# Where the loads of the value weights stand among the attention's transpositions

## The chip, the cores and the metric

The kernel runs on one core of a Trainium2 chip. The metric is the device time of one execution in microseconds (us), taken as the median of several runs. TensorE (PE in the profile), VectorE (DVE), ScalarE (ACT), GpSimd (POOL) and SyncE (SP) each run their own instructions in order; SP does nothing but issue DMAs.

## The reference

Two pre-norm residual layers over 1024 positions of width 1024, then an RMS norm. The first layer is a gated linear recurrence. The second is attention with a forget gate, and the change lies in it:

```python
u = h @ w_in
q, k, v, gate = ...                        # 16 heads of 64
cum = cumsum(log_sigmoid(f_logit + b_f))   # per head, over positions
logits = q @ k.T / 8 + (cum[q] - cum[k])   # causal
p = softmax(logits)
y = (p @ v) * silu(gate)
x = x + y @ w_out
```

## The kernel before

The attention layer works through the 16 heads one by one, each in two halves of 512 query positions. For a head and a half, `maxima` (L941) makes the scores `S` of four blocks of 128 queries on TensorE, adds the mask and takes the maximum on VectorE (L965), takes the exponential `p` on ScalarE (L970), scales it into two fp16 parts `pp` (ScalarE L978, VectorE L979) and has SP issue a DMA that transposes `pp` into `pT` (L982). So a run of `maxima` has four transpositions. `weigh` (L988) multiplies `pT` with the values into `O`; its first product needs all four transpositions of its half.

`run` (L1034) interleaves such generators by a string of digits and dots: a digit advances a generator (0 is `weigh`, 1 is `maxima`), a dot advances `fill`, the projections that make queries, keys and gates of later heads (`gps`), and `side`, which moves keys and queries into the operands `T` and `U` by DMA (`pieces`, L823, four DMAs for a batch). For each head there are two runs. The second (L1289) weighs the second half of this head and makes the scores of the first half of the next head; its order is

```python
ORDER = "1.1..1.1..00", "1.1.1.1...0000"
```

The values of four heads at a time are made by `values` (L695), for three groups behind the first: after the heads 3, 7 and 11 it is passed to the second run as `vals`, and what is left of it runs when that run is over (`drain(vals)`, L1299). These are the places 1, 2 and 3. The weights of a group come in four tiles of 256 KB from `in_wv`, for k = 0, 2, 4 and 6: `load_v` fetches one into a buffer `wf` (three of them, shared with all weights of the layer, L118), and `cast_v` makes two fp16 parts `w16` of it, the high one on ScalarE and the low one on VectorE (`cast16`, L641). The products go to `vps`: 192 of 128x256, for eight tiles of 128 tokens; the first four token tiles stand in an order that lets work begin with the first weight tiles (L731). A finished token tile is evicted in two halves, each by ScalarE and VectorE (`v`, L761 and L762). Token tiles 0, 2, 4 and 6 use the two banks "g" of PSUM in turn, tiles 1, 3, 5 and 7 the two banks "S", which the scores use too.

Before the change, `run` advances `vals` at three steps: at step 1 (three loads), at step 5 (two casts and the fourth load) and at the last digit 1 (two casts).

The order of instructions on each engine is made by a scheduler when the kernel is built, from the order of the code and its own estimates. `tc.issue_after(i)` keeps what is issued inside behind the instruction `i`. `turns` holds all transpositions so far, so at step 0 of the second run `turns[-1]` and `turns[-2]` are the last two transpositions of the run that has just ended, and at step 1 `turns[-1]` is the first of the new run. `behind` (L1042) keeps the later transpositions behind the fourth load, and the first part of `O`'s eviction (L1010) behind the last cast.

Of the kernel before, what the change touches and what calls it, by code (L numbers as in the profile page):

```python
# [40 lines left out]
def trunk(ctx: ExitStack, tc: tile.TileContext, xt, w0, wg, wo0, pc, gn, gf, w1, wv, wf, bf, wo1, out):  # L41
# [26 lines left out]
    def matmul(*args, **kw):  # L68
        pe[0] = nc.tensor.matmul(*args, **kw)  # L69
        return pe[0]  # L70
# [25 lines left out]
    def to_hi(hi, src, eng, scale=None):  # L96
        if eng is nc.scalar:
            if scale is None:
                cast_last[0] = nc.scalar.copy(hi, src)
            else:  # L100
                nc.scalar.activation(hi, src, AF.Copy, scale=scale)
        elif eng is nc.gpsimd:
            nc.gpsimd.tensor_scalar(hi, src, 1.0 if scale is None else scale, 0.0, ALU.mult, ALU.add)
        elif scale is None:
            eng.tensor_copy(hi, src)
        else:
            eng.tensor_scalar(hi, src, scale, None, ALU.mult)
# [41 lines left out]
    def drain(gen):  # L149
        for _ in gen:  # L150
            pass

    def take(gen, n):
        for _ in range(n):
            next(gen, None)
# [43 lines left out]
    with nullcontext(ExitStack()) as l0:  # L199
# [45 lines left out]
        k = 0  # L245
# [374 lines left out]
    with ExitStack() as l1:  # L620
# [13 lines left out]
        def load16(src, shape, b):  # L634

            wt = loaded(shape)
            for part, sl in src:
                fetch(wt[:, :, sl], part)
            return wt, b

        def cast16(wt, b):  # L641

            n = wt.shape[1]
            both = wpool.tile([P, 2, *wt.shape[1:]], FP16, tag=next(slots), name="w16")
            hi, lo = both[:, 0], both[:, 1]
            cast_last[0] = nc.scalar.activation(hi, wt, AF.Copy, scale=scales[:, b : b + 1])
            nc.vector.scalar_tensor_tensor(lo, wt, scales[:, b : b + 1], hi, ALU.mult, ALU.subtract)
            return [(hi[:, k], lo[:, k]) for k in range(n)]
# [46 lines left out]
        def values(g):  # L695

            ex = HEADS if g == 0 else 0
            parts, raw = [], []

            def load_v(k):  # L700
                src = [(wv[g, :, k : k + 2], slice(0, 256))]
                if ex:
                    src.append((wf[:, k : k + 2], slice(256, 256 + ex)))
                raw.append(load16(src, (2, 256 + ex), g))

            def cast_v(n=1):
                for _ in range(n):
                    parts.extend(cast16(*raw.pop(0)))

            if ex:  # L710
                for k in range(0, KT, 2):
                    load_v(k)
                    if k % 4:
                        cast_v(2)
                    if k == 2:
                        yield
            else:
                for k in range(0, 6, 2):
                    load_v(k)
                yield  # L720
                with tc.issue_after(seen[0].ins):
                    cast_v(2)
                load_v(6)
                yield
                cast_v(2)
                yield
            Vs[2 * g], Vs[2 * g + 1] = [], []
            todo = [(st, k) for st in range(8) for k in range(KT)]
            if not ex:

                todo[: 2 * KT] = [(st, k) for h in range(2) for st in range(2) for k in range(h * 4, h * 4 + 4)]  # L731
            pts = {}
            for st, k in todo:
                if k == 0:
                    if st % 2:
                        pt = ps.tile([P, SEQ], F32, tag="S", name="vps")[:, : 256 + ex]
                    else:
                        pt = ps.tile([P, 256 + ex], F32, tag="g", name="vps")
                    pts[st] = pt
                pt = pts[st]  # L740
                c = (st % 4) * P
                xh, xl = hT[st // 4][k]
                wh, wl = parts[k]
                xh, xl = xh[:, c : c + P], xl[:, c : c + P]
                matmul(pt, xh, wh, start=k == 0, stop=False)
                matmul(pt, xl, wh, start=False, stop=False)
                matmul(pt, xh, wl, start=False, stop=k == KT - 1)
                if k % 4 == 1:
                    yield
                if k < KT - 1:  # L750
                    continue
                if ex and st < 4:
                    take(splitting, 2)
                if True:
                    if ex:
                        nc.vector.tensor_scalar(fz[:, st], pt[:, 256:], rf[:, st : st + 1], None, ALU.mult)
                    for a in range(2):
                        v = vpool.tile([P, 4, HD], FP16, tag=f"v{st}", name=f"v{st}", bufs=2)
                        src = pt[:, a * P : (a + 1) * P].rearrange("p (b d) -> p b d", b=2)
                        rv_ = rv[:, g, st : st + 1]  # L760
                        to_hi(v[:, 0::3], src, nc.scalar, scale=rv_)  # L761
                        nc.vector.scalar_tensor_tensor(v[:, 1:3], src, rv_, v[:, 0::3], ALU.mult, ALU.subtract)  # L762
                        Vs[2 * g + a].append(v)
# [53 lines left out]
        turns = []  # L817
# [41 lines left out]
        def forget(half):  # L859
# [24 lines left out]
            for hd in range(2):  # L884
                if half == 0:
                    load(hd, cs, (0,) if hd == 0 else ())

        first = values(0)
        next(first)
        next(first)  # L890
# [143 lines left out]
        def run(order, *gens, fill=iter(()), side=iter(()), vals=None):  # L1034

            for n, i in enumerate(order):
                if vals and n in (1, 5):
                    with tc.issue_after(turns[-1].ins):
                        next(vals)
                if vals and n == order.rfind("1"):  # L1040
                    next(vals)
                    behind[:] = loaded_last[0], cast_last[0]  # L1042
                with tc.issue_after(pe[0].ins):
                    next(fill if i == "." else gens[int(i)], None)
                if i == ".":
                    next(side, None)
            for g in gens:
                drain(g)
# [196 lines left out]
        load(0, halves[1], (1,))  # L1245
        load(1, halves[1], (1,))
        run("00.0.0", maxima(0, 0), fill=fill)
        load_q(1, 0)
        drain(fill)
        for hd in range(HEADS):  # L1250
# [23 lines left out]
            if hd == HEADS - 1:  # L1274
                first = "1..1.0.1.0.1..."
            side = chain(pieces(hd + 1, 0, 0), pieces(hd + 1, 0, 1)) if hd else iter(())
            run(first, weigh(hd, 0), maxima(hd, 1), fill=fill, side=side)
            drain(side)
            if hd == HEADS - 1:
# [6 lines left out]
            if hd == 14:  # L1286
                side = chain(side, late())
            vals = values(hd // 4 + 1) if hd % 4 == 3 and hd < 12 else None
            run(second, weigh(hd, 1), maxima(hd + 1, 0), fill=fill, side=side, vals=vals)  # L1289
            behind.clear()  # L1290
            drain(side)
# [88 lines left out]
```

## Time and profile before

| | |
|---|---|
| three runs | 1066.57, 1062.53 and 1066.17 us, median 1066.17 |
| the profiled execution | 1067.16 us, span of its instructions 1065.4 us |
| busy in the span | PE 1028.7 us (97%), DVE 784.2 (74%), ACT 659.9 (62%), POOL 92.2 (9%) |
| granted TensorE clock, mean | 0.993 |
| DMA | 148.92 MB in 219805 packets, 161936 of them under 512 bytes |
| value products `vps` | 768, of which 192 in each of the places 1 to 3 |

Times in the profile count from the span's start. A line of the timeline gives start, duration, engine, source line, operation, what is written and read, shape, count, and in brackets how long the engine was idle before and what ended that. SPq is SP's queue of DMA issues; the duration there is that of the issuing, not of the transfer. L57, L66 and L69 are helper lines through which all of ScalarE's activations, the loads and all matmuls go, so groups are told apart by their tiles.

### The profile page before, as it was taken

The numbers are of one execution on the slowest core, as the hardware profiler recorded it, in microseconds if no ns is written. First come the engines' busy times: TensorE is split into PE (matmuls) and PEld (weight loads), VectorE is DVE, ScalarE is ACT, GpSimd is POOL, SyncE is SP. The second block draws the span as 40 slices with busy tenths as digits, with TensorE's granted clock in tenths as the row PEclk, the third lists the DMA queues.
The fourth block names the chain that finished last, engine by engine and source line by source line (L and its number), as shares of the span: only waits on it lengthen the run. The fifth ranks groups of instructions, "written<-read, shape, count | busy, mean of one in ns | idle before, by whom it ended". The sixth has DMA issues, their size and how long they took to land. (4 is left out here: it accounts for less than half of the span.)

```text
span 1065.4 us, 15063 instructions
## 1 busy us (share of the span) xinstructions
PE 1028.7 (97%) x5094; PEld 721.8 (68%) x5094; DVE 784.2 (74%) x1456; ACT 659.9 (62%) x1211; POOL 92.2 (9%) x87
## 2 busy tenths in 40 slices
PE   9999999999999999998999989999999989999997
PEld 6787878888888888765445556554755448577776
DVE  7789667667856868885878866888487874986575
ACT  8479666565656575567657655675466664764455
POOL 1311111012103110001000000000000000012100
PEclk9999999999999999999999999999999999999999
DMA  7112434233423311543688993998658984789984
GB/s 244 60 49 63 117 88 128 78 114 112 134 65 121 112 58 40 170 130 87 150 163 171 180 198 80 192 179 176 163 106 180 180 190 120 151 194 240 250 199 159
DMA packets 219805, 148.92 MB, mean 140 GB/s; under 512 B 161936, under 2 KB 174864, under 8 KB 219728
## 3 DMA queue, kind: packets, MB, share of 16 engines
q1 hardware_dynamic: 217328, 140.09, 54.2%
q0 software_dynamic: 2400, 7.87, 2.4%
q8 instruction: 40, 0.66, 0.3%
q14 instruction: 37, 0.30, 0.1%
HBM read 73.33 MB, written 11.67 MB: 80 GB/s over the span
## 5 line engine op out<-in xcount | busy, mean ns | idle before, releaser
L69 PE MATMUL gps<-h,w 128*128 128x512 f16 x1152 | 269.1, 380 | 1.3 <-DVE qkl L795 1.1
L69 PEld LDWEIGHTS <-w 128*128 128x128 f16 x1152 | 104.2, 98 | 126.4 <-issue 13.8
L57 ACT ACTIVATE p<-S,m 128x128 f32<-128x128 f32 (+7 forms) x128 | 94.5, 739 | 68.1 <-DVE m L965 30.6
L57 ACT ACTIVATE pp<-p,sums 128x128 f16<-128x128 f32 (+7 forms) x128 | 96.0, 769 | 34.7 <-DVE sums L977 18.5
L979 DVE SCALAR_TENSOR_TENSOR pp<-p,sums,pp 128x128 f16<-128x128 f32 (+7 forms) x128 | 102.5, 813 | 14.1 <-ACT pp L57 11.7
L69 PE MATMUL S<-T,U 96*128 96x512 f32 (+7 forms) x384 | 106.2, 385 | 5.0 <-ACT p L57 4.7
L69 PE MATMUL vps<-w,h 128*128 128x256 f16 (+1 forms) x768 | 92.3, 282 | 12.7 <-ACT w L57 8.3
L965 DVE CUSTOM_DVE_ANT_0 S<-S,mask 128x128 f32<-128x128 f32 (+7 forms) x128 | 96.9, 758 | 6.1 <-PE S L69 5.3
L110 POOL TENSOR_TENSOR wl<-wf,wh 128x512 fp32r<-128x512 f32 x46 | 70.9, 1545 | 324.3 <-ACT wh L57 254.3
L69 PEld LDWEIGHTS <-h 128*128 128x128 f16 x768 | 76.7, 101 | 28.0 <-issue 10.8
L69 PEld LDWEIGHTS S<-T,U 128*128 128x128 f32 (+1 forms) x384 | 67.7, 190 | 28.8 <-ACT p L57 13.6
L57 ACT CAST wh<-wf 128x512 fp32r<-128x512 f32 x88 | 51.7, 593 | 53.6 <-PE ops L69 27.1
L69 PE MATMUL ops<-yh,wh 128*128 128x512 f32 x192 | 76.8, 400 | 0.9 <-ACT yh L57 0.5
L69 PE MATMUL ups<-hh,wl 128*128 128x512 f32 x192 | 75.8, 395 | 1.8 <-POOL wl L110 1.8
L69 PE MATMUL ups<-hh,wh 128*128 128x512 f32 x192 | 76.4, 399 | 0.7 <-ACT hh L57 0.6
L69 PE MATMUL O<-pT,v 128*128 128x512 f16 (+3 forms) x396 | 71.0, 322 | 6.0 <-DMA pT<-pp 6.0
L69 PE MATMUL gps<-hh,wh 128*128 128x512 f32 x192 | 75.7, 394 | 0.8 <-ACT wh L57 0.8
L69 PE MATMUL ups<-hl,wh 128*128 128x512 f32 x192 | 76.1, 396 | 0.1
L69 PE MATMUL ops<-yh,wl 128*128 128x512 f32 x192 | 75.7, 394 | 0.1
L69 PE MATMUL gps<-hh,wl 128*128 128x512 f32 x192 | 75.5, 393 | 0.0
L69 PE MATMUL gps<-hl,wh 128*128 128x512 f32 x192 | 75.5, 393 | 0.0
L69 PE MATMUL ops<-yl,wh 128*128 128x512 f32 x192 | 74.6, 394 | 0.0
(196 smaller groups left out, 1883.5 us busy)
## 6 DMA issues: line engine op xcount, KB each, us to landing
wf<-in_w SPq DMA_DIRECT2D x106, 256.0 KB
wsf<-in_w SPq DMA_DIRECT2D x48, 256.0 KB
wf<-in_wo SPq DMA_DIRECT2D x64, 128.0 KB
T<-qkh SPq DMA_DIRECT2D x64, 128.0 KB
U<-qkh SPq DMA_DIRECT2D x64, 128.0 KB
x<-in_xt SPq DMA_DIRECT2D x16, 256.0 KB
wsf<-in_wv SPq DMA_DIRECT2D x16, 256.0 KB
x1d<-x SPq DMA_DIRECT2D x16, 256.0 KB
```

The source lines that it names most:

```text
L57: act[0] = op(*args, **kw)
L69: pe[0] = nc.tensor.matmul(*args, **kw)
L110: return eng.tensor_tensor(lo, src, f32(hi), ALU.subtract)
L965: nc.vector.tensor_tensor_reduce(S[:, :n], S[:, :n], mask[:, SEQ - n :], -1.0, -NEG, ALU.add, ALU.min, accum_out=m)
L979: nc.vector.scalar_tensor_tensor(both[:, :, 1], p, r, both[:, :, 0], ALU.mult, ALU.subtract)
```

## The change

`values` gives way once more: two tiles are loaded, then the third. `run` advances it twice at step 0, where the first two loads are kept behind the last transposition but two of the ended run (`turns[-3]`) and the third load behind its last one (`turns[-1]`), and no longer at step 1. The steps 5 and "last digit 1" stay. The casts' place is left to the scheduler as before, at the steps in which they stood.

```diff
             else:
-                for k in range(0, 6, 2):
-                    load_v(k)
+                load_v(0)
+                load_v(2)
+                yield
+                load_v(4)
                 yield
                 with tc.issue_after(seen[0].ins):
                     cast_v(2)
...
             for n, i in enumerate(order):
-                if vals and n in (1, 5):
+                if vals and n == 0:
+                    with tc.issue_after(turns[-3].ins):
+                        next(vals)
+                    with tc.issue_after(turns[-1].ins):
+                        next(vals)
+                if vals and n == 5:
                     with tc.issue_after(turns[-1].ins):
                         next(vals)
```

What becomes of this on the engines, at place 1 (places 2 and 3 read alike). First SP's queue: `pT_5294` is the ended run's, `pT_5425` (now `pT_5431`) the new run's; the loads of value weights are those from `in_wv`, and `in_w1` are the projection weights that follow. Before:

```order
L66 DMA U0_4064<-qkl_3833 64x512
L982 DMA_TRANSPOSE pT_5294<-pp_5366 128x14x128
L982 DMA_TRANSPOSE pT_5294<-pp_5387 128x16x128
L66 DMA T1_4062<-cumd_3779 2x512
L66 DMA T1_4062<-qkh_3792 64x512 x2
L66 DMA T1_4062<-qkl_3793 64x512
L982 DMA_TRANSPOSE pT_5425<-pp_5433 128x2x128
L66 DMA wf_5439<-in_wv 128x512
L66 DMA wf_5441<-in_wv 128x512
L66 DMA wf_5443<-in_wv 128x512
L982 DMA_TRANSPOSE pT_5425<-pp_5463 128x4x128
L982 DMA_TRANSPOSE pT_5425<-pp_5484 128x6x128
```

Now the same stretch of SP's queue:

```order
L66 DMA U0_4064<-qkl_3833 64x512
L66 DMA wf_5424<-in_wv 128x512
L66 DMA wf_5426<-in_wv 128x512
L984 DMA_TRANSPOSE pT_5294<-pp_5366 128x14x128
L984 DMA_TRANSPOSE pT_5294<-pp_5387 128x16x128
L66 DMA T1_4062<-cumd_3779 2x512
L66 DMA wf_5428<-in_wv 128x512
L66 DMA T1_4062<-qkh_3792 64x512 x2
L66 DMA T1_4062<-qkl_3793 64x512
L984 DMA_TRANSPOSE pT_5431<-pp_5439 128x2x128
L984 DMA_TRANSPOSE pT_5431<-pp_5463 128x4x128
L66 DMA T1_4062<-cumd_3779 2x512
```

Two loads moved in front of the ended run's last two transpositions, and the third moved into the first batch of keys. Behind this, the second batch of keys now stands in front of the new run's third transposition, the fourth load (`wf_5496`) behind it, then the fourth transposition and the two weight tiles that follow:

```order
L66 DMA T1_4062<-qkh_3792 64x512 x2
L66 DMA T1_4062<-qkl_3793 64x512
L984 DMA_TRANSPOSE pT_5431<-pp_5484 128x6x128
L66 DMA wf_5496<-in_wv 128x512
L984 DMA_TRANSPOSE pT_5431<-pp_5523 128x8x128
L66 DMA wf_5543<-in_w1 128x512
L66 DMA wf_5545<-in_w1 128x512
```

Before, the fourth load followed the third transposition directly, and the second batch of keys stood behind it. Next, ScalarE's order at the same place; `w16_5490`, `w16_5493`, `w16_5510` and `w16_5513` are the four value weight tiles, `w16_5547` and `w16_5556` the two that follow, `v0` to `v3` the evictions of token tiles 0 to 3. Before:

```order
L57 ACTIVATE pp_5523<-p_5521,sums_5424 128x4x128
L57 ACTIVATE w16_5490<-wf_5439,wsq_238 128x512
L57 ACTIVATE w16_5493<-wf_5441,wsq_238 128x512
L57 ACTIVATE w16_5510<-wf_5443,wsq_238 128x512
L57 ACTIVATE w16_5513<-wf_5496,wsq_238 128x512
L57 ACTIVATE yo_5271<-O_5559,wsq_238 64x512
L57 ACTIVATE w16_5547<-wf_5543,wsq_238 128x512
L57 ACTIVATE v0_5620<-vps_5582,rv_3464 128x2x64
L57 ACTIVATE v1_5638<-vps_5595,rv_3464 128x2x64
L57 ACTIVATE w16_5556<-wf_5545,wsq_238 128x512
```

And now:

```order
L57 ACTIVATE w16_5510<-wf_5428,wsq_238 128x512
L57 ACTIVATE p_5521,sums_5430<-S_5516,m_5519 128x512
L57 CAST qkh_3792<-gps1_5501 128x512
L57 ACTIVATE pp_5484<-p_5482,sums_5430 128x3x128
L57 ACTIVATE pp_5523<-p_5521,sums_5430 128x4x128
L57 ACTIVATE w16_5513<-wf_5496,wsq_238 128x512
L57 ACTIVATE yo_5271<-O_5559,wsq_238 64x512
L57 ACTIVATE w16_5547<-wf_5543,wsq_238 128x512
L57 ACTIVATE w16_5556<-wf_5545,wsq_238 128x512
L57 ACTIVATE v0_5620<-vps_5582,rv_3464 128x2x64
L57 ACTIVATE v1_5638<-vps_5595,rv_3464 128x2x64
L57 ACTIVATE v0_5623<-vps_5582,rv_3464 128x2x64
```

The first three casts moved in front of the fourth exponential (`p_5521`), directly behind the third; the cast `w16_5556` moved in front of the first evictions. VectorE's half of each cast and eviction moved in the same way. Last, TensorE's products around the first use of the fourth weight tile, `w16_5513`, behind 53 products of the place before:

```order
L69 MATMUL vps_5595<-w16_5510,h16_3522 128x256
L69 LDWEIGHTS h16_3519
L69 MATMUL vps_5644<-w16_5493,h16_3519 128x256
L69 LDWEIGHTS h16_3523
L69 MATMUL vps_5582<-w16_5513,h16_3523 128x256
```

And now, behind 72:

```order
L69 MATMUL vps_5675<-w16_5510,h16_3522 128x256
L69 LDWEIGHTS h16_3522
L69 MATMUL vps_5675<-w16_5510,h16_3522 128x256
L69 LDWEIGHTS h16_3523
L69 MATMUL vps_5582<-w16_5513,h16_3523 128x256
```

All products of token tiles 0 to 3 (`vps_5582`, `vps_5595`, `vps_5644`, `vps_5675`) with the first three weight tiles now come ahead of the fourth, and token tile 0 is complete after 84 of the 96 products instead of 65.

## The prediction

> **What bounds the kernel now.** I read the page first, then the list of all waits, then TensorE's timeline around the three places where values are computed, then the timelines of ScalarE and of SP's queue there.
>
> ```profile
> span 1065.4 us, 15063 instructions
> ```
>
> ```profile
> ACT w L57 <- DMA wf<-in_wv: 15.5, 8, 3.0
> PE vps L69 <- ACT w L57: 8.3, 3, 3.5
> ```
>
> The first row is from the page, the other two are from the waits (sum in us, times, longest). TensorE is the engine that sets the end, so only its idle or slowed time counts. Of its waits, three before the value products (vps) make 8.3 us: it waits for ScalarE's casts (w), and these wait for value weights (wf from in_wv) to land.
>
> ```profile
> 620.09 2.99 PE L69 MATMUL O<-pT,v 128*128 128x512 f16 x16
> 625.73 10.64 PE L69 MATMUL vps<-w,h 128*128 128x256 f16 x96 [2.66 <-ACT w L57]
> 637.11 10.65 PE L69 MATMUL vps<-w,h 128*128 128x256 f16 x96 [0.74 <-DVE v L762]
> ...
> 745.29 2.98 PE L69 MATMUL O<-pT,v 128*128 128x512 f16 x16
> 750.45 12.31 PE L69 MATMUL vps<-w,h 128*128 128x256 f16 x96 [2.18 <-ACT w L57]
> 762.95 10.65 PE L69 MATMUL vps<-w,h 128*128 128x256 f16 x96 [0.19 <-DVE v L762]
> ...
> 871.82 2.98 PE L69 MATMUL O<-pT,v 128*128 128x512 f16 x16
> 878.28 23.98 PE L69 MATMUL vps<-w,h 128*128 128x256 f16 x192 [3.48 <-ACT w L57]
> ```
>
> These are places 1, 2 and 3 (start, length, count, idle time before). Each has 192 products, 96 for token tiles 0 to 3 and 96 for 4 to 7; undisturbed, 96 take 10.65 us, 0.111 each. The waits in front are 2.66 + 2.18 + 3.48 = 8.32 us, those before token tile 4 are 0.74 + 0.19 = 0.93. Besides, place 2 took 12.31 for its first 96, 1.66 too long, and place 3 23.98 for 192, 2.68 too long. Why, this row by windows shows (columns: busy time by engine, then granted clock, DMA share, GB/s):
>
> ```profile
> 751.00:754.50 3.50, 3.50 (x19) 2.44 (x17) 1.62 (x3) 1.05 (x2) 0.00 (x0) 0.51 0.90 188
> 877.30:884.20 6.90, 5.92 (x29) 4.07 (x28) 2.99 (x5) 3.51 (x5) 0.00 (x0) 0.51 0.97 220
> ```
>
> The granted clock is 0.51 there: after the waits of 2.18 and 3.48 TensorE ran at half speed for a while; after the 2.66 of place 1 it did not. So the three places lose 8.32 + 0.93 + 1.66 + 2.68 = **13.6 us**. This is the ceiling of the change.
>
> The Trainium skill ("TensorE: Matmul & The Clock Gate", section "What's actually happening") lets the clock fall after an idle window of about 3.4 us that runs independently of the kernel. By that rule the wait of 2.18 would not halve the clock, place 2 would keep its 1.66, and the gain below would be 6.3 instead of 8.0 us, 1059.9. The trace does not agree: the clock was 0.51 right after 2.18 us.
>
> **The change part by part.** Nothing is computed more or less; the same loads, casts and products stand in another order. I call the value weight tiles V0, V2, V4, V6, the ending run's last two transpositions R3 and R4, the new run's N1 to N4, and the next two weight tiles W1, W2.
>
> *Removed: the wait in front.* These are ScalarE's casts in place 1:
>
> ```profile
> 624.96 0.72 ACT L57 ACTIVATE w<-wf,wsq 128x512 f16<-128x512 f32 x1 [1.81 <-DMA wf<-in_wv]
> 625.93 1.51 ACT L57 ACTIVATE w<-wf,wsq 128x512 f16<-128x512 f32 x2 [0.24 <-DMA wf<-in_wv]
> 630.36 0.72 ACT L57 ACTIVATE w<-wf,wsq 128x512 f16<-128x512 f32 x1 [2.92 <-DMA wf<-in_wv]
> ...
> 633.73 0.72 ACT L57 ACTIVATE w<-wf,wsq 128x512 f16<-128x512 f32 x1 [1.94 <-DMA wf<-in_w]
> 634.36 0.61 ACT L57 ACTIVATE v<-vps,rv 128x128 f16<-128x128 f32 x2
> 634.85 0.72 ACT L57 ACTIVATE w<-wf,wsq 128x512 f16<-128x512 f32 x1
> ```
>
> And these are SP's issues there:
>
> ```profile
> 612.83 5.07 SPq L982 DMA_TRANSPOSE pT<-pp  x2
> 618.00 0.39 SPq L66 DMA_DIRECT2D T<-cumd  x1
> ...
> 620.29 1.20 SPq L982 DMA_TRANSPOSE pT<-pp  x1
> 621.53 1.53 SPq L66 DMA_DIRECT2D wf<-in_wv  x3
> ...
> 626.50 0.34 SPq L66 DMA_DIRECT2D wf<-in_wv  x1
> ...
> 630.55 1.67 SPq L66 DMA_DIRECT2D wf<-in_w  x3
> ```
>
> V0, V2 and V4 are issued from 621.53 and cast from 624.96, about 3.4 us later. In front of R3 (612.83) V0 and V2 land by about 616; V4, issued behind R4 at about 618.5, lands by 622. The casts stand in front of the fourth exponential, and V0 and V2 are cast before TensorE ends O at 623.1 (620.09 + 2.99). V4 is first needed 24 products (2.7 us) into vps. So the front waits go entirely, and with them the half speed: 8.32 + 1.66 + 2.68 = 12.66 of the 13.6. The three casts now hold up the fourth exponential and the cast of the next keys by 3 x 0.7 = 2.1 us. What hangs on these, N3, N4 and the keys' low half on VectorE, is wanted by the next run only; the bank of the fourth scores is wanted by token tile 3, 54 products (6.0 us) into vps. That hides it.
>
> *Added: R3 and R4 stand behind two loads.* O (weigh of the run's second half) needs both. The casts of V0 and V2 began 0.97 apart, and V4 followed within 0.87 (the row x2 has no gap), so two loads take the DMA engines some 1.8 us. How much of it reaches O is read from these windows (the last column but one is the DMA share) and one wait:
>
> ```profile
> 613.00:614.00 1.00, 0.81 (x5) 0.20 (x2) 1.00 (x3) 0.97 (x4) 0.00 (x0) 1.00 0.00 0
> 744.00:744.50 0.50, 0.50 (x4) 0.26 (x3) 0.50 (x3) 0.00 (x0) 0.00 (x0) 1.00 0.51 99
> 870.50:871.00 0.50, 0.50 (x4) 0.24 (x3) 0.50 (x3) 0.00 (x0) 0.00 (x0) 1.00 0.69 129
> ```
>
> ```profile
> 620.09 2.82 PEld L69 LDWEIGHTS <-v 128*128 128x128 f16 x16 [0.39 <-DMA pT<-pp]
> ```
>
> In place 1 the DMA engines idle for the whole microsecond before R3's data (share 0.00), which takes 1.0 of the 1.8; O already waits 0.39 for R4, so the other 0.8 is added. In places 2 and 3 the engines are busy ahead of R3, and I read the dip of the share at 744.0 to 744.5 and 870.5 to 871.0 as the end of R4; O began at 745.29 and 871.82, 0.8 to 0.9 later. 1.8 less this is 0.9 each. Sum: 0.8 + 0.9 + 0.9 = **2.6 us**. No row shows a load ahead of these transpositions, so I bound it: nothing (if R4 is delayed by less than its slack) and, from above, 1.8 us of data and two issues of 0.5 (1.53 for three) with no slack, 2.8 a place, 8.4 in all. I take the working from the shares, which are its nearest rows. R3's issue itself is late by at most those two 0.5.
>
> *Moved: V6.* In the new order it is needed after 72 products instead of 53: 72 x 0.111 = 8.0 us after vps begins. SP must first issue, from R4's end, the first batch of keys with N1 (618.00 to 621.49, 3.5 us), V4 (0.5) and N2 (1.2), and then the second batch with N3 (3.5 again): 8.8 with gaps. Place 1: 617.90 + 0.8 + 8.8 = 627.5 is V6's issue, against 626.50 before. Its cast began 3.86 after its issue (626.50, 630.36) and takes 0.72: 632.1. TensorE asks for it at 623.1 + 0.8 + 8.0 = 631.9, and stands 0.2 to 0.4. Places 2 and 3 take their R4 end from these rows:
>
> ```profile
> 738.10 4.43 SPq L982 DMA_TRANSPOSE pT<-pp  x2
> 755.24 1.50 SPq L66 DMA_DIRECT2D wf<-in_w  x3
> ```
>
> ```profile
> 864.61 3.95 SPq L982 DMA_TRANSPOSE pT<-pp  x2
> 883.09 1.51 SPq L66 DMA_DIRECT2D wf<-in_w  x3
> ```
>
> Place 2: 742.53 + 0.9 + 8.8 + 4.6 = 756.8 against 748.3 + 0.9 + 8.0 = 757.2; place 3: 868.56 + 14.3 = 882.9 against 874.8 + 8.9 = 883.7. No wait. Sum **0.4**; bounds are 0 and, with the 4.30 us of W1 in place 2 (755.24 to 759.54) as latency, 0.9 in total.
>
> *Moved: both casts of W1 and W2 stand ahead of the first eviction* (before: one of them stood behind two evictions). Token tile 4 needs the bank of tile 0, whose two evictions are ScalarE's first and third behind W2's cast. W1's issue follows V6 by 0.34 and N4, 1.8 in all: 629.3, 754.0, 880.1, that is 1.2, 1.2 and 3.0 earlier than the rows show. I let the casts come earlier by as much. W1's began at these times:
>
> ```profile
> 759.54 0.72 ACT L57 ACTIVATE w<-wf,wsq 128x512 f16<-128x512 f32 x1 [3.29 <-DMA wf<-in_w]
> 886.09 0.72 ACT L57 ACTIVATE w<-wf,wsq 128x512 f16<-128x512 f32 x1 [2.10 <-DMA wf<-in_w]
> ```
>
> W2's follows by 1.2 (633.73 to 634.85) and ends 0.72 later; three evictions by 0.3 and VectorE's half add 1.3: 3.2 us from W1's cast to tile 4. Place 1: 633.73 - 1.2 + 3.2 = 635.7, and the 96 products end at 623.9 + 0.4 + 10.65 = 634.9. Place 2: 761.6, products done at 759.8. Place 3: 886.3, products done at 886.35. Waits 0.8 + 1.8 + 0 = **2.6 us** in place of the old 0.93; bounds are 0, and the first rival's, if the casts come no earlier.
>
> **Sum.** 13.6 - 2.6 - 0.4 - 2.6 = **8.0 us** gained. By places, tile 4 begins at 635.7 instead of 637.11, at 761.6 instead of 762.95 and at 886.4 instead of 891.61 (902.26, where the row of 23.98 ends, less 10.65): 1.4 + 1.3 + 5.2. Behind tile 4 the stages are the same and SP's queue has drained, so I take the shift to last. The profiled execution took 1067.16 (span 1065.4 and 1.8 around it); it would take 1059.2. It lies 1.0 above the median 1066.17, so on the scale of the median I predict **1058.2**.
>
> **The rivals.** *Given back at tile 4.* The front wait goes, but the loads of W1 and W2 land when they did, since the DMA engines hold the same data. Tile 4 then begins 3.2 after the old cast: 636.9, 762.7, 889.3, a gain of 0.2 + 0.2 + 2.3 = 2.7 us: 1063.5. For it: these casts waited 1.94, 3.29 and 2.10 for DMA. Against it: SP issues them earlier, and V0 to V4 are out of the way by then. Chance 0.27.
>
> *Slower: the transpositions pay in full.* R3 and R4 took SP 5.07 us together where N1 took 1.20: they fill the queue. If the two loads hold both up for 2.8 us in each place, O's wait passes the 2.2 us after which place 2 lost its clock, and half speed costs 1.66 to 2.68 more, 2.2 in the mean: 3 x 5.0 = 15.0, with 3.0 for V6 and tile 4, 18.0 against 13.6, 1070.6. It decides from about 2.2 us of lateness on, and with 3.1 it passes 1071.5. For it: the DMA share is at or over 1 in these stretches. Against it: the idle microsecond of place 1 and the slack of 0.8 in the others. Chance 0.15, two thirds of it beyond 0.5%. The Trainium skill ("DMA: Bandwidth & Descriptors", section "Queues, rings and completion order") says that each DMA engine consumes a queue's descriptors in ring order; by it the loads' whole 1.8 us is passed on, which no row shows yet.
>
> *More than forecast:* the delays hide altogether: 13.6, 1052.6. For it: only O's slack and the landing of W2 stand in between. Chance 0.08.
>
> **How the numbers follow.** The forecast has 0.50 and spans 1055 to 1060.8. A measurement of this kernel tells about 0.5% (5.3 us) from no change: 1060.8 to 1071.5. Faster: 0.50 + 0.08 = 0.58; within: 0.27 and a third of 0.15, 0.32; slower: the other 0.10. The range reaches from 1053.5, near the ceiling, to 1065.5, which holds the first rival and all bounds of R4's delay short of the clock's fall (8.0 - 5.8 = 2.2 gained); the slow rival's 0.15 and a little of the ceiling stay out.
>
> **What would show it.** Right, if TensorE goes from O to vps with no wait for casts and with a clock of 1.00 in all three places, O waits about 1 us for pT, and tile 4 waits 1 to 2 us for evictions behind W2's cast. Wrong, if vps still waits for ACT w in front, if O waits over 2 us and the clock falls, or if tile 4 begins where it did.

## The result, and the profile after

The changed kernel took 1071.16 us (median of 20 runs, 1065.4 to 1074.88), the kernel before beside it 1063.2 (20 runs, 1060.34 to 1068.01). The ratio is 1.0054, 95% interval 1.0039 to 1.0069: 5.8 us slower at 1066 us. The two medians lie further apart, 8.0 us, because each kernel's executions spread over 8 to 10 us; I go by the ratio. Measured again (the run after_again below) it was 1.0066 (1.0046 to 1.0086). The prediction was 1058.2, a gain of 8.0 on the 1066.17 of the first three runs.

From the page and the waits of the changed kernel (sum in us, times, longest):

```profile
span 1069.4 us, 15059 instructions
```

```profile
PE vps L69 <- DVE v L764: 11.7, 6, 3.3
PE O L69 <- DMA pT<-pp: 7.8, 7, 1.9
...
PE vps L69 <- ACT w L57: 4.5, 3, 2.2
```

Most of the value products' waiting is no longer for casts (ACT w, 8.3 before, 4.5 now) but for evictions (DVE v, 11.7 here, tile 4 and others together; 4.2 before). TensorE's timeline at the three places, in the columns of the prediction:

```profile
619.64 2.99 PE L69 MATMUL O<-pT,v 128*128 128x512 f16 x16 [1.49 <-DMA pT<-pp]
622.46 8.02 PE L69 MATMUL vps<-w,h 128*128 128x256 f16 x72
631.79 2.78 PE L69 MATMUL vps<-w,h 128*128 128x256 f16 x24 [1.30 <-ACT w L57]
637.12 10.65 PE L69 MATMUL vps<-w,h 128*128 128x256 f16 x96 [2.56 <-DVE v L764]
...
746.83 2.97 PE L69 MATMUL O<-pT,v 128*128 128x512 f16 x16 [1.10 <-DMA T<-cumd]
749.63 8.02 PE L69 MATMUL vps<-w,h 128*128 128x256 f16 x72
759.83 2.78 PE L69 MATMUL vps<-w,h 128*128 128x256 f16 x24 [2.17 <-ACT w L57]
765.93 13.42 PE L69 MATMUL vps<-w,h 128*128 128x256 f16 x96 [3.32 <-DVE v L764]
...
878.25 2.99 PE L69 MATMUL O<-pT,v 128*128 128x512 f16 x16 [1.86 <-DMA pT<-pp]
881.08 8.02 PE L69 MATMUL vps<-w,h 128*128 128x256 f16 x72
890.08 2.78 PE L69 MATMUL vps<-w,h 128*128 128x256 f16 x24 [0.98 <-ACT w L57]
895.39 10.65 PE L69 MATMUL vps<-w,h 128*128 128x256 f16 x96 [2.54 <-DVE v L764]
```

Each place has the same four rows. The first 72 products follow O with no wait: the wait in front is gone. In its place stand three others: O waits for its transpositions (the row of place 2 names T from cumd, the transfer that came last by the profile; R4 stands just ahead of it on SP), the last 24 of the first 96 products wait for V6's cast, and tile 4 waits for an eviction. Two windows show the price of the 13.42. The first covers the wait for V6 in place 2, the second tile 4's first products; the clock is the last column but two:

```profile
757.00:760.00 3.00, 0.83 (x9) 0.60 (x7) 0.19 (x1) 0.92 (x2) 0.00 (x0) 1.00 1.00 224
764.80:771.60 6.80, 5.67 (x27) 4.08 (x28) 2.29 (x8) 2.11 (x7) 0.00 (x0) 0.50 0.46 136
```

In the first window the clock was still 1.00. Behind the waits of 2.17 and 3.32 it was 0.50 for 6.8 us, which cost 13.42 - 10.65 = 2.77. So the places lose 4.45 for O, 4.45 for V6, 8.42 at tile 4 and 2.77 for the clock: **20.1 us** where the kernel before lost 13.6. These 6.5 us more agree with the 5.8 of the ratio, whose interval is 4.2 to 7.4 us. The spans of the two profiled executions differ by less, 4.0 us (1069.4 and 1065.4), since the stretches between the places also differ from one execution to the next.

### The profile page after: what moved, and what is told of

Its sections match the earlier page's. It is cut to its first block, busy times and chain, and to the rows that moved or that the text cites. A ratio compares the mean times of both kernels' runs of the same rounds, so it can differ in the third digit from the quotient of the medians.

```text
span 1069.4 us, 15059 instructions
## 1 busy us (share of the span) xinstructions
PE 1027.7 (96%) x5094; PEld 721.8 (67%) x5094; DVE 784.2 (73%) x1456; ACT 659.0 (62%) x1211; POOL 93.4 (9%) x87
## 5 line engine op out<-in xcount | busy, mean ns | idle before, releaser
L69 PE MATMUL vps<-w,h 128*128 128x256 f16 (+1 forms) x768 | 91.1, 279 | 16.3 <-DVE v L764 11.7
L647 DVE SCALAR_TENSOR_TENSOR w<-wf,wsq,w 128x512 f16<-128x512 f32 (+1 forms) x74 | 54.6, 748 | 33.0 <-ACT w L57 32.5
```

## The experiments

My theory after this reading: the three waits have three causes. R3 and R4 stand behind two loads (O). V6's load stands behind the second batch of keys and N3 (V6). The casts of W1 and W2 stand ahead of the first evictions on ScalarE and wait there for their loads (tile 4). The main rival: it is one cause, the loads ahead of R3, and all that follows on SP's queue slides with them.

All sums in this table are worked out from the rows of TensorE's timeline of one execution, as above; "more" is the sum less the 13.6 of before; "measured" is the ratio less 1, times 1066 us.

| kernel | O | casts | tile 4 | clock | sum | more | ratio (95%) | measured |
|---|---|---|---|---|---|---|---|---|
| before | 0 | 8.3 | 0.9 | 4.3 | 13.6 | | | |
| changed | 4.5 | 4.5 | 8.4 | 2.8 | 20.1 | 6.5 | 1.0054 (1.0039 to 1.0069) | 5.8 |
| after_again | 3.3 | 4.4 | 9.0 | 3.0 | 19.7 | 6.1 | 1.0066 (1.0046 to 1.0086) | 7.0 |
| e1_behind | 0 | 2.1 | 8.8 | 0 | 10.9 | -2.7 | 1.0037 (1.0013 to 1.0060) | 3.9 |
| e3_wcast | 5.1 | 4.1 | 2.1 | 0 | 11.3 | -2.3 | 0.9982 (0.9959 to 1.0006) | -1.9 |
| e6_dummy | 3.0 | 3.2 | 3.1 | 1.7 | 11.0 and 4.0 of work | 1.4 | 1.0025 (1.0001 to 1.0049) | 2.7 |
| e7_front | 4.7 | 3.4 | 5.4 | 0 | 13.5 | -0.1 | 1.0002 (0.9976 to 1.0028) | 0.2 |
| e8_behindw | 0.2 | 2.6 | 1.7 | 0 | 4.4 | -9.2 | 0.9923 (0.9900 to 0.9946) | -8.2 |
| e5_all | 0 | 3.0 | 0 | 0 | 3.0 | -10.6 | 0.9915 (0.9893 to 0.9938) | -9.1 |
| e9_bw | 0 | 7.8 | 0 | 1.5 | 9.3 | -4.3 | 0.9970 (0.9955 to 0.9984) | -3.2 |
| e10_pool | 1.7 | 4.2 | 7.1 | 1.7 | 14.6 | 1.0 | 1.0031 (1.0013 to 1.0049) | 3.3 |
| e11_poolgate | 1.9 | 4.1 | 6.7 | 1.6 | 14.3 | 0.7 | 1.0050 (1.0027 to 1.0072) | 5.3 |
| e12_both | 3.2 | 4.3 | 0 | 0 | 7.6 | -6.0 | 0.9940 (0.9914 to 0.9966) | -6.4 |

("Casts" holds every wait inside the first 96 products.) In nine of the twelve lines with a ratio the waits at the three places account for the measured difference within 1.6 us; e1_behind, e10_pool and e11_poolgate are worse than their sums by 6.6, 2.3 and 4.6. Two things limit the table. It leaves out what lies between the places: the stretch from tile 4 of one place to O's readiness in the next takes 107 to 112.5 us in these profiles, so the difference of two profiled spans and that of their sums lie up to 4.4 us apart. And each edit lets the scheduler place the neighbours anew: in e1_behind, for instance, N1 and N2 also moved ahead of half of the first batch of keys.

**e3_wcast: the casts of W1 and W2 behind the evictions.**

```diff
-        plan = []
+        plan, evicted = [], []
...
-                for i, _ in enumerate(gemm_steps(pt, zip(w.cast(), hT[h]))):
+                with tc.issue_after(evicted[0].ins) if evicted else nullcontext():
+                    parts = w.cast()
+                for i, _ in enumerate(gemm_steps(pt, zip(parts, hT[h]))):
...
                         to_hi(v[:, 0::3], src, nc.scalar, scale=rv_)
+                        if not ex and st == a == 1:
+                            evicted[:] = [act[0]]
...
-                        u["load"], u["cast"] = 2, (2, 3)
+                        u["load"], u["cast"] = 2, ()
```

> The changed kernel, with the casts of W1 and W2 put behind the eviction of token tile 1 on ScalarE; loads and products stand as they do. My theory: the wait at tile 4 (2.56, 3.32, 2.54 us) came from these two casts, which waited for their loads ahead of the first evictions. Without them tile 0's bank needs its products (done 12 products, 1.33 us, before the 96 end) and three evictions by 0.31 with VectorE's half, 1.3 us: wait 0 to 0.6 in each place, and no half clock in place 2, so 8.42 - 1 + 2.77, some 8 to 10 us less than the changed kernel: 1061 to 1064. O's wait and V6's stay (4.45 each). Rival A (the wait at tile 4 is the evictions' own chain: tile 0 is complete only after 84 of 96 products): wait stays 1.5 us or more in each place, time 1067 to 1071. Rival B (given back: the casts, now later, hold up the next head's scores or the filling products behind the value products): the wait at tile 4 goes, but new waits of 2 to 3 us stand behind the value products, time 1068 to 1072.

It took 1064.74 us beside 1066.32 of before. TensorE in place 2, then ScalarE in place 1:

```profile
748.70 8.02 PE L69 MATMUL vps<-w,h 128*128 128x256 f16 x72
758.62 2.78 PE L69 MATMUL vps<-w,h 128*128 128x256 f16 x24 [1.90 <-ACT w L57]
762.10 10.65 PE L69 MATMUL vps<-w,h 128*128 128x256 f16 x96 [0.70 <-DVE v L768]
```

```profile
634.56 0.80 ACT L57 ACTIVATE v<-vps,rv 128x128 f16<-128x128 f32 x2 [0.85 <-PE vps L69]
635.72 1.14 ACT L57 ACTIVATE v<-vps,rv 128x128 f16<-128x128 f32 x4 [0.36 <-DVE v L768]
636.74 1.35 ACT L57 ACTIVATE w<-wf,wsq 128x512 f16<-128x512 f32 x2
```

The evictions now wait for TensorE's products and VectorE's half of them, the two casts behind them wait for nothing, and tile 4 waits 0.70 in each place instead of 2.56, 3.32 and 2.54. The clock stays at 1.00 in all three. That is 6.3 + 2.8 = 9.1 us, and from the changed kernel's ratio to this one's it is 7.7. So about 6 us of the tile 4 wait were these two casts; the 0.70 left, a little over the 0 to 0.6 expected, is the evictions' own chain. Rival A falls. Rival B falls by the time (1064.74, not 1068 to 1072), but the profile does not clear it wholly: this execution took 1067.85, its span is only 3.3 us shorter than the changed kernel's, and from the last tile 4 to the end it took 177.5 us, 174.0 in the changed kernel. Whether the later casts have a part in that is open; of the two kernels below with the same edit of the casts, e8_behindw took 173.5 there and e5_all 177.0.

**e9_bw: the same edit on the kernel before (the control).**

> The kernel before, with the casts of W1 and W2 behind the eviction of token tile 1 (the control for e3_wcast). My theory: before, only one of these casts held up the first evictions by a wait, and tile 4 waited 0.74, 0.19 and 0 us; the front wait for V0 to V6 (8.3 us) and the half clock behind it stay: ratio 0.998 to 1.002. Rival (these casts behind the evictions are a gain of their own, whatever the order of the loads): ratio 0.992 to 0.996, as e3_wcast won against the changed kernel.

1063.41 us beside 1066.15: a gain of 0.3%, a little more than I expected and less than the rival's. Tile 4's old waits of 0.74 and 0.19 are gone, and the front waits of 2.71, 2.29 and 2.75 stay. The casts behind the evictions are a small gain of their own (3.2 us by the ratio); of the 7.7 that e3_wcast won against the changed kernel, the larger part had been given away by the change.

**e1_behind: no load ahead of R3 and R4.**

```diff
                 if vals and n == 0:
-                    with tc.issue_after(turns[-3].ins):
+                    with tc.issue_after(turns[-1].ins):
                         next(vals)
```

> The changed kernel, but V0 and V2 are loaded behind R4 (with V4) instead of ahead of R3: no load stands ahead of the last two transpositions. My theory (three waits took the place of the old front wait: O's for R3 and R4 behind two loads, 1.49 + 1.10 + 1.86 = 4.45 us; the cast of V6, 4.45 us; token tile 4 behind the casts of W1 and W2, 8.42 us; and 2.77 us of half clock): O's wait falls to 0.5 or less in each place, 3 to 4 us in all; V0 is now issued about where O begins, lands some 3.5 us later and is cast in 0.7, so vps waits 0.5 to 1.5 us in front in each place; the waits for V6 and at tile 4 stay at 1 to 3 us each. Time 1067 to 1072, no gain over before. Rival (the loads ahead of R3 and R4 are the whole trouble, since all behind them on SP's queue slides with them): the waits for V6 and at tile 4 go to under 1 us as well, time 1058 to 1062.

1069.7 us beside 1066.32. TensorE in place 3, then SP's row of R3 and R4 in place 1:

```profile
875.63 2.98 PE L69 MATMUL O<-pT,v 128*128 128x512 f16 x16
878.45 8.01 PE L69 MATMUL vps<-w,h 128*128 128x256 f16 x71
887.12 2.91 PE L69 MATMUL vps<-w,h 128*128 128x256 f16 x25 [0.66 <-ACT w L57]
892.79 10.65 PE L69 MATMUL vps<-w,h 128*128 128x256 f16 x96 [2.76 <-DVE v L764]
```

```profile
611.57 5.29 SPq L984 DMA_TRANSPOSE pT<-pp  x2
```

O waits no more, so its wait came from the two loads. V6's wait is 0.85, 0.58 and 0.66, half of the changed kernel's and under the 1 to 3 that I expected: here the rival was right, and a part of V6's lateness came from the loads ahead of R3. But tile 4 still waits 2.89, 3.16 and 2.76, so the rival of one cause for all falls. I had expected 0.5 to 1.5 us in front of vps, and there is none: V0 and V2 need not be ahead of R3 at all, only ahead of the keys. The sum at the places says 2.7 us faster than before, the ratio says 3.9 slower. The profiled execution itself, at 1068.86, shows where some 4 us of this lie: between the places 1 and 2, in the O of a later head. Its row in e1_behind with the clock there, then the same O before:

```profile
722.76 4.63 PE L69 MATMUL O<-pT,v 128*128 128x512 f16 x16 [3.24 <-DMA pT<-pp]
```

```profile
722.70:730.00 7.30, 7.24 (x31) 3.95 (x32) 2.84 (x5) 2.78 (x5) 0.00 (x0) 0.77 0.71 144
```

```profile
720.81 2.99 PE L69 MATMUL O<-pT,v 128*128 128x512 f16 x16 [2.01 <-DMA pT<-pp]
```

That is 1.2 us more of waiting and 1.6 of a lowered clock, and the O ahead of it (at 694.77) waits 1.22 where no such wait stands before. Whether the edit causes these waits is not shown: e8_behindw, with the loads in the same place, waits 0.31 and 2.12 at these two and keeps its clock. The other executions of e1_behind were not traced.

**e8_behindw and e5_all: the edits together.** e8_behindw is e1_behind with e3_wcast's edit; e5_all also loads V6 earlier:

```diff
-                if vals and n == 5:
+                if vals and n == 3:
```

> The first two experiments together: V0, V2 and V4 loaded right behind R4 (none ahead of R3), and the casts of W1 and W2 behind the eviction of token tile 1. My theory (the terms of the changed kernel are separate, each with its own cause): O waits under 0.4 us, vps has no wait in front (e1_behind showed none), V6's cast costs 0.6 to 0.9 and tile 4 about 0.7 in each place: 4 to 5 us in all at the three places, against 9.25 us of waits and 4.34 us of half clock in the profiled run of before. 8 to 9 us less than before, ratio 0.990 to 0.995. Rival (what is won at the places comes back between them, as O's waits for transpositions in the next heads, 3.24 us at 722.76 in e1_behind): ratio 0.997 to 1.002.

> As the kernel before it, with V6 loaded two steps of the run earlier as well, ahead of the second batch of keys. My theory: V6's wait (0.6 to 0.9 us a place) goes too, for its load is some 3 us earlier; N3, N4 and the keys behind it have slack. Left are about 0.7 us at tile 4 in each place; ratio 0.988 to 0.993. Rival (V6's buffer or the keys and N3 behind it become late: the next head's scores wait for T, or its O for N3): V6's wait goes, but 1 to 2 us come back per place behind the value products, ratio as the kernel before or up to 0.004 above it.

1057.66 and 1057.49 us beside 1066.15: both are 8 to 9 us faster than the kernel before, by the ratios, as expected of the first. TensorE in place 1 of e8_behindw:

```profile
619.48 2.99 PE L69 MATMUL O<-pT,v 128*128 128x512 f16 x16 [0.17 <-DMA pT<-pp]
622.30 7.91 PE L69 MATMUL vps<-w,h 128*128 128x256 f16 x71
630.93 2.91 PE L69 MATMUL vps<-w,h 128*128 128x256 f16 x25 [0.71 <-ACT w L57]
634.40 10.65 PE L69 MATMUL vps<-w,h 128*128 128x256 f16 x96 [0.56 <-DVE v L768]
```

and in place 3 of e5_all:

```profile
865.83 4.09 PE L69 MATMUL vps<-w,h 128*128 128x256 f16 x36
870.92 1.69 PE L69 MATMUL vps<-w,h 128*128 128x256 f16 x14 [1.00 <-DVE qkl L110]
873.20 15.69 PE L69 MATMUL vps<-w,h 128*128 128x256 f16 x142 [0.59 <-ACT w L57]
```

The front wait, O's and the clock's cost are gone together, and the casts of W1 and W2 no longer count. The gain that I had forecast lay there. Loading V6 earlier won nothing that can be measured, against what I expected: TensorE's order now asks for it after 50 products instead of 71, and waits 0.50, 0.86 and 0.59 again. (When V6 is asked for is the scheduler's choice; the order at L731 interleaves token tiles 0 and 1 only, not four.) The 1.00 of place 3 ended with VectorE's qkl, which reads a tile `gps`; that the value products wait for its bank is read from the names (both are of the banks "g") and not shown by a run.

**e12_both: V0 and V2 ahead of R3, the rest as in e5_all.** It differs from e5_all by the edit of e1_behind alone.

> The changed kernel (V0, V2 ahead of R3) with V6 loaded two steps earlier and the casts of W1 and W2 behind the eviction of tile 1: it differs from e5_all (1057.49 us) only in where V0 and V2 are loaded, so it prices the loads ahead of R3 and R4 by themselves. My theory: O waits 1.1 to 1.9 us in each place, 4 to 5 us in all, and nothing is won for it, since vps has no wait in front in e5_all either; V6 waits 0 to 0.9 us, tile 4 none or 0.7: 1061 to 1063.5. Rival (with V6 and the casts out of the way the delay of R3 and R4 is hidden, or the earlier casts of V0 and V2 let the rest start earlier): 1056 to 1059.

1061.81 us beside 1064.97; 0.9940 against 0.9915 for e5_all, 2.7 us, with intervals that overlap. O's rows:

```profile
621.28 2.99 PE L69 MATMUL O<-pT,v 128*128 128x512 f16 x16 [1.07 <-DMA pT<-pp]
...
744.79 2.97 PE L69 MATMUL O<-pT,v 128*128 128x512 f16 x16 [1.48 <-DMA T<-cumd]
...
869.86 2.99 PE L69 MATMUL O<-pT,v 128*128 128x512 f16 x16 [0.68 <-DMA pT<-pp]
```

3.2 us, less than the 4 to 5 expected but of that kind, and V6 waits 0, 2.20 and 1.39, more than expected. So the two loads ahead of R3 cost 4.6 us by the sums (7.6 - 3.0) and 2.7 by the ratios, the latter not clear of noise, and no row shows a gain from them.

**e7_front: V0 and V2 ahead of R3, V4 where it was before.**

```diff
+                if vals and n == 0:
+                    with tc.issue_after(turns[-3].ins):
+                        next(vals)
                 if vals and n in (1, 5):
```

(on the kernel before, with V0 and V2 as a step of their own)

> One part of the change alone: V0 and V2 are loaded ahead of R3, but V4 stays where it was before, behind N1, and V6 too. My theory: O's wait is as in the changed kernel (1.1 to 1.9 us a place), since it is these two loads that delay R3 and R4; V4 lands later than in the changed kernel, and vps waits 0 to 1 us for it after some 30 products; V6 and the casts of W1 and W2 come as late as in the changed kernel or up to 0.5 us later: 1071 to 1075. Rival (it is V4 behind R4, ahead of the keys and N1 to N3, that makes V6 and W1, W2 late): V6 and tile 4 wait under 1 us each, and the time is 1060 to 1064.

1067.15 us beside 1066.32. My 1071 to 1075 was a miss, and the rival's 1060 to 1064 as well. O waits as expected (1.49, 1.27, 1.93), but tile 4 waits less:

```profile
637.58 10.65 PE L69 MATMUL vps<-w,h 128*128 128x256 f16 x96 [1.75 <-DVE v L764]
...
763.33 10.65 PE L69 MATMUL vps<-w,h 128*128 128x256 f16 x96 [1.58 <-DVE v L764]
...
889.69 10.65 PE L69 MATMUL vps<-w,h 128*128 128x256 f16 x96 [2.07 <-DVE v L764]
```

Here V4's load stands behind N1, and only three of the four transfers of the second batch of keys are ahead of N3 and V6; SP issues V6 4.0 us after the first value product in place 1, 5.0 in the changed kernel. So V4 directly behind R4, the other half of the change, makes some 5 to 7 us of its loss: 1.0002 against 1.0054 and 1.0066, and 13.5 against 20.1 in the sums.

**e6_dummy: twelve idle products more in each place.** They begin token tile 3's sum anew each time, so nothing of them remains in it.

```diff
                     pts[st] = pt
+                    if not ex and st == 3:
+                        for i in range(12):
+                            matmul(pt, hT[0][0][0][:, i * 32 : i * 32 + P], parts[0][0], start=True, stop=True)
```

> The changed kernel with 12 idle products more in each place (each begins tile 3's sum anew, so that they drop out; 36 in all, 0.111 us each, 4.0 us of TensorE's time). My theory: in each place TensorE waits for W1's and W2's casts before tile 4 (2.56, 3.32, 2.54 us), so 1.33 us more work ahead of it disappears in that wait: the wait at tile 4 falls by 1.0 to 1.4 us in each place, tile 4 begins when it did, and the time stays within 1 us of the changed kernel's; as TensorE idles less in place 2, the clock may stay at 1.00 there, and then the time is 2 to 3 us lower. 1068 to 1072. Rival (TensorE's own work or its order sets tile 4): tile 4 begins 1.33 us later in each place, 4 us more, 1074 to 1076.

1069.84 us beside 1066.32, a ratio 0.0029 below the changed kernel's, though TensorE had 4.0 us more to do. In place 2:

```profile
763.01 3.87 PE L69 MATMUL vps<-w,h 128*128 128x256 f16 x34 [2.38 <-ACT w L57]
767.87 10.65 PE L69 MATMUL vps<-w,h 128*128 128x256 f16 x96 [0.99 <-DVE v L767]
```

From O's start to tile 4 it is 17.64, 18.29 and 16.72 us (places 1 to 3); in the changed kernel 17.48, 19.10 and 17.14. Tile 4 begins no later, to within 0.2 us, with 1.33 us more work ahead of it, so TensorE's work does not set it. In place 2 the wait of 3.32 became 0.99 and the clock stayed at 1.00 there; in place 3 it fell ahead of the value products, behind a wait of 2.17 for O, and cost 1.7.

**e10_pool and e11_poolgate: V0 and V2 on GpSimd's queue.** What of two loads delays R3 and R4, their place in SP's queue or their data?

```diff
-                load_v(0)
-                load_v(2)
+                ready = nc.gpsimd.tensor_copy(gated_[:], gate[:, 7:8])
+                loads_by[0] = nc.gpsimd
+                with tc.issue_after(ready.ins):
+                    load_v(0)
+                    load_v(2)
+                loads_by[0] = nc.sync
...
```

(e11_poolgate, where `gate` is the tile of the ending run's sums, handed to `values`; e10_pool is without the copy and its wait.)

> The changed kernel with V0 and V2 issued on GpSimd's queue instead of SP's, ahead of R3 as far as their buffers allow. It tells apart what delays R3 and R4. If it is their place behind the loads in SP's own queue: O's wait falls from 1.49, 1.10, 1.86 to 0.5 us or less in each place, vps has no wait in front, and V6's wait falls with it; time 2 to 5 us less than the changed kernel, 1066 to 1069. If it is the data of the loads on the DMA engines, whichever queue they stand in: O's wait stays at 1 to 1.9 us a place, time 1070 to 1073.

> The changed kernel with V0 and V2 both issued on GpSimd's queue, behind a copy of one column that is ready when the ending run's last exponential is summed (in e10_pool one of them went out some 15 us earlier, so that run left the question open). Both now go out shortly before R3, beside SP's queue instead of in it. If the place in SP's own queue delays R3 and R4: O's wait is 0.6 us or less in each place (1.49, 1.10, 1.86 in the changed kernel), and R3 and R4 occupy SP for about the 5.2 us of e1_behind instead of 6.2. If it is the loads' data on the DMA engines: O waits 1.0 to 1.9 us a place and R3 and R4 occupy SP for 6 us. Time 1066 to 1070 by the first, 1069 to 1073 by the second; the casts of W1 and W2 still cost their 2 to 3 us a place at tile 4 by both.

e10_pool took 1069.64 us beside 1066.15, with waits of 0.51, 0.59 and 0.55 for O. It tells the two apart badly, for only one load went out beside R3; the other's buffer was free, and GpSimd issued it long before. e11_poolgate took 1070.77 beside 1064.97; GpSimd and SP in place 1:

```profile
610.35 1.26 POOL L66 DMA_DIRECT2D wf<-in_wv  x2 [0.60 <-ACT w L57]
```

```profile
611.88 6.30 SPq L989 DMA_TRANSPOSE pT<-pp  x2
```

R3 and R4 occupy SP for 6.30 us here with no load ahead of them in its queue, as in the changed kernel (6.21) and not as in e1_behind (5.29). O waits 1.07, 0.68 and 0.18. So a part of the delay is the loads' data on the DMA engines, whatever the queue. The rest of O's wait went with the loads' place in SP's queue, where their two issues alone take 1.06 us in place 1. Neither theory holds alone, and how the two share the delay stays open. The Trainium skill ("DMA: Bandwidth & Descriptors", section "Queues, rings and completion order") says that a DMA engine takes turns between the queues that have work for it; the 6.30 us agree with that.

**after_again: the changed kernel once more.** There is no edit.

> The changed kernel itself, once more, beside these two and the kernel before on one chip. My theory: as first measured, ratio 1.004 to 1.007, with waits of 1 to 3.5 us for O, V6 and tile 4 in each place; the places where the clock falls may differ from one execution to the next, so the half clock need not be in place 2. Rival (the first profile was a chance one): the waits at tile 4 are under 1 us, or the ratio is under 1.002.

1072.52 us beside 1064.97. All three waits are there again in all three places (O 1.18, 1.17, 0.90; V6 1.27, 1.36, 1.78; tile 4 2.95, 3.32, 2.76), and this time the clock fell in places 2 and 3. So the waits are not a chance of one execution; where the clock falls is.

## Why the prediction was wrong, point by point

**The wait in front: right.** It went entirely, with the half speed behind it; e9_bw, with the loads where they were, has both still (half speed in place 3). But e1_behind shows that it goes as well with V0, V2 and V4 directly behind R4, so the loads ahead of R3 won none of it. And the 4.34 us of half clock in the 13.6 belong to one execution, at 1067.16, 4 us over the later median of 1063.2; in e9_bw much the same front waits cost 1.5 of clock. So the ceiling of 13.6 was itself on the high side.

**R3 and R4 behind two loads: right in kind, too small.** 0.8 + 0.9 + 0.9 = 2.6 forecast; 4.45 measured (3.25 in after_again), within the bound of 8.4.

**The failed step: V6.** "No wait. Sum 0.4" was 4.45. I moved V6's issue with O's start and let SP take 8.8 us from R4's end to V6. SP's rows of place 2 and ScalarE's behind them:

```profile
739.64 5.59 SPq L984 DMA_TRANSPOSE pT<-pp  x2
...
755.57 0.58 SPq L66 DMA_DIRECT2D wf<-in_wv  x1
...
757.54 1.06 SPq L66 DMA_DIRECT2D wf<-in_w  x2
```

```profile
759.05 0.72 ACT L57 ACTIVATE w<-wf,wsq 128x512 f16<-128x512 f32 x1 [6.52 <-DMA wf<-in_wv]
...
762.44 1.47 ACT L57 ACTIVATE w<-wf,wsq 128x512 f16<-128x512 f32 x2 [1.96 <-DMA wf<-in_w]
763.82 0.61 ACT L57 ACTIVATE v<-vps,rv 128x128 f16<-128x128 f32 x2
765.12 1.93 ACT L57 ACTIVATE v<-vps,rv 128x128 f16<-128x128 f32 x6 [0.69 <-DVE v L764]
```

R4's issue ends at 745.23, 1.6 us before O starts (746.83); before, it ended 2.76 before O. So SP was held for 1.2 us more than O was, and my 0.9 for O was wrongly taken for SP's delay too. From there to V6's issue (755.57) it took 10.3, not 8.8. N3 alone held SP for 2.52 there, 1.27 in the two other places. The 1.2 and 1.5 make V6 2.7 us late beside O, and the wait is 2.17. In the places 1 and 3 R4's end to V6 took 9.87 and 9.83, V6 was 1.2 and 2.2 late beside O, and the waits are 1.30 and 0.98. What each transfer ahead of V6 has to do with it is read from these rows; no run took them away one by one.

**The failed step: tile 4.** 2.6 forecast, 8.42 measured, the largest miss. "I let the casts come earlier by as much": they didn't. In place 2 W1 is issued at 757.54, and its cast starts 4.90 us later (4.30 before). Beside O's start that is 15.6 us, forecast 12.15: the 2.7 of V6, 0.2 between the two issues, and 0.6 of latency. In the places 1 and 3 it is 13.9 and 13.2, forecast 11.6 and 10.4, and before 13.6 and 14.3. Both casts now stand ahead of both evictions of tile 0 and hold them up; e3_wcast took them out of the way and 6.3 us of the 8.42 went.

**The clock: a term that I left out.** In the sum I let the half clock go with the wait in front and did not ask whether the new waits bring it back; only the slow rival priced it, and only for O. In place 2 they did, for 2.77: the last two waits there, 2.17 and 3.32, are as long as the 2.18 that halved it before, and longer.

**The rivals.** "Given back at tile 4" named the place and the two casts, and by its condition (W1 and W2 land no earlier) the time would be 1063.5. In place 2 they landed later than before, since SP issued them later; V6, the larger delay of R3 and R4 and the clock came on top. "Slower: the transpositions pay in full" gave 1070.6, close to the time but by another way: O's wait in the changed kernel never passed 1.86. Of the conditions for "wrong", the last came true, and more: tile 4 begins where it did or later, at 637.12, 765.93 and 895.39, before at 637.11, 762.95 and 891.61.

## What to carry to other kernels

A load that is issued earlier on a full queue pushes every later one back, so follow each of them to the instruction that waits for it: here the price was paid some 25 us later, by two casts that no line of the change names. An in-order engine should not hold a cast that waits for a transfer ahead of the evictions that free a bank; putting two of them behind those evictions took 7.7 us off the changed kernel here, which brought it back to the time of before (ratio 0.9982, interval up to 1.0006). And a list of waits removed is half a sum: each new wait is asked for its own clock, its own place in the queue and its own latency.

## What the runs showed of the hardware

TensorE's clock fell behind several shorter waits: 2.17 and 3.32 us with 2.78 of work between them were followed by 6.8 us at 0.50, and in after_again 1.36 and 3.32 by 1.59 us of loss. No single wait in these two was longer than 3.32. Single waits of about 2 us were enough elsewhere: 1.98 in e11_poolgate (at 850.33) and 2.08 in e6_dummy (at 723.12), each for an O, were followed by a clock of 0.64 and 0.65 over the next 4.7 and 4.9 us. But 2.01 before (at 720.81) and, in e1_behind, 0.58 and 3.16 in place 2 were followed by none, so the length of a wait alone does not tell. The Trainium skill ("TensorE: Matmul & The Clock Gate", section "What's actually happening") asks for an idle window of some 3.4 us; the runs here show the fall with less idle time than that in one piece. Executions of one kernel differ with the clock: of the changed kernel's 20, the eight under 1068 us had a mean granted clock of 0.997, the twelve over 1070 us 0.9945, which would be 2.7 of the 5.7 us between them. The clock is not all of it: in e1_behind the execution with 0.998 took 1068.86 us, and one with 0.994 took 1067.55.

R3 and R4 keep SP longer when two loads of 256 KB are in flight: 6.21, 5.59 and 5.52 us at the places of the changed kernel, 5.29, 4.14 and 4.36 in e1_behind, 6.30, 6.26 and 5.47 with the loads in another engine's queue.
